# A recurrent mixer's decays from a second scan instead of reciprocals, and its conditioning vectors multiplied on VectorE

## The chip, the cores and the metric

The kernel runs on one core of one Trainium2 chip and computes a whole two-layer block in one launch. The metric is the device time of one execution in microseconds (us). Engines are named as in the profile: PE is TensorE's matmuls, PEld its weight loads, DVE is VectorE, ACT is ScalarE, POOL is GpSimd, SP is SyncE, which here only issues DMAs.

## What is computed

512 tokens of width 1024 pass through two layers, each with a mixer and a feed-forward part. The mixer of layer 0 is recurrent, that of layer 1 is dilated attention. Each layer has six conditioning vectors of 1024 numbers, `cond @ ada_w[layer] + ada_b[layer]`, which shift, scale and gate the norms. The parts that matter here:

```python
cond = jax.nn.silu(c)                                  # one row of 1024
mod = (cond @ ada_w[layer] + ada_b[layer])             # six vectors of 1024
sh1, sc1, g1, sh2, sc2, g2 = jnp.split(mod, 6, axis=-1)
u = rms_norm(h, norm_g[layer, 0]) * (1.0 + sc1) + sh1
# recurrent mixer, 8 heads of 128, chunks of C = 32 tokens
log_f = jnp.log(lb + (1.0 - lb) * jax.nn.sigmoid(f_raw))
k = (1.0 - lb) * jax.nn.sigmoid(-f_raw)
q = jax.nn.silu(q_raw)
b = jnp.cumsum(log_f, axis=2)                          # within a chunk
q_dec = q * jnp.exp(b)
k_inv = k * jnp.exp(-b)
a = jnp.where(causal, q_dec @ k_inv.T, 0.0)            # within a chunk
k_end = k * jnp.exp(b_last - b)                        # b_last: end of the chunk
o = a @ v + q_dec @ state
state = jnp.exp(b_last) * state + k_end.T @ v
o = rms_norm(o) * norm_g * silu(g)                     # per head
return o @ w_out
```

## The kernel before, in words

Matmuls with weights are done in fp32 precision from three products of rounded halves: each weight tile is split into `hi` (a cast on ACT, L113) and `lo` (raw minus hi on DVE, L114), and each tile of activations into `uh` and `ul`; the products uh·hi, ul·hi and uh·lo are L599, L600 and L601. One such matmul covers 128x512.

The weights come as one stream of 1 MB tiles called `raw` (class `Stream`), in an order fixed in the program. SP issues the loads in that order (L85). There are **two raw buffers**: the load of a tile waits until every reader of the tile two places ahead of it has finished. For a weight tile the readers are the hi cast and the lo subtraction; for a chunk of `ada_w` (512 of its rows by 512 columns, "conditioning chunk" below) they are whatever multiplies it with `cond`. The parts hi and lo have three buffers.

During the mixer of layer 0 the stream holds 12 weight tiles of the mixer (per pair of heads one of f, one of q, one of g) and, woven between them, 12 conditioning chunks of layer 0 (vectors 2, 3 and 4; each vector has two halves of 512 columns, each half two chunks: `ada_chunk(l, v, hf, kq)`), then the first chunks of layer 1. In the names of the trace and of the order below, raw0, 1, 3, 5, 9, 13, 15, 19, 23, 26, 30, 34 are the weight tiles f0, q0, f1, q1, g0, f2, q2, g1, f3, q3, g2, g3; raw2, 4 and 6, 8 are the two halves of vector 2, raw10, 12 and 14, 17 those of vector 4, raw18, 21 and 22, 25 those of vector 3; raw27 is the first chunk of layer 1.

`ada_groups` (L383 to L401) multiplies a chunk of layer 0 on PE: per chunk two records of four matmuls, each with a column tile of 32 (L395), 8 matmuls in all; after the second chunk ACT copies the sum from PSUM to `shared` (L399). Layer 1's chunks go the other way, `ada_chunk`'s own code: four DVE instructions per chunk (L415 for the first, L417 for the rest), each `shared += raw[:, k] * cond[k]`, 128x512. The sum over partitions is later made on PE with a column of ones (L444) and finished on DVE (L433, L435).

The mixer's loop goes over four pairs of heads. Per pair, `block` makes f and q (L599 to L601), ACT applies the sigmoids, then per head `head_prep` (L1503 to L1546) computes on DVE the decays inside chunks: a scan over 512 columns (L1510), the reciprocal of its 512 columns (L1516), products with K and Q (L1517 to L1519), 12 small steps of 4 or 16 elements (L1525 to L1536) and two products of 256 columns (L1542, L1543); two more products per head are on POOL (L1541, L1544). `core_a` to `core_d` (L1548 to L1603) are the head's matmuls; the output `on` of a head is written by DVE (L1595, tile aT) and transposed by PE in core_d (L1602). `gate_pair` makes g and multiplies the output (L1611, L1613). `fl` (Fillers) hands out these steps between blocks of the next weights, core_a to core_d two to five ticks behind `head_prep`.

The order on each engine is then set by a list scheduler with its own estimates of durations, not by hand; each engine runs its instructions in the order so fixed.

Of the kernel before, what the change touches and what calls it, by code (L numbers as in the profile page):

```python
# [37 lines left out]
SEEN = lambda t: t.rearrange("p (x n a) -> p x a n", a=2, n=P)  # L38
PLACED = lambda t: t.rearrange("p (x a n) -> p x a n", a=2, n=P)
# [276 lines left out]
def block_kernel(tc, x, c, positions, ada_w, ada_b, norm_g, hgrn_w_in, lower, hgrn_norm_g, hgrn_w_out,  # L316
                 attn_w_in, attn_w_out, ffn_w_in, ffn_w_out, inv_freq, out):
    nc = tc.nc
    act, dve, pool, pe = nc.scalar, nc.vector, nc.gpsimd, nc.tensor
    x2, out2 = x[0], out[0]  # L320
    V4 = lambda t: t.rearrange("p (a b) -> p a b", a=4)
# [3 lines left out]
    with ExitStack() as ctx:  # L325
# [48 lines left out]
        accs = {}  # L374
# [11 lines left out]
        def ada_groups(l, v, hf, kq):  # L386


            def run(raw):
                if kq == 0:  # L390
                    accs[l, v, hf] = bank("mm")
                ps, r = accs[l, v, hf], V4(raw)
                for k in range(4):
                    j = slice(32 * k, 32 * k + 32)
                    pe.matmul(ps[j], cond_tiles[:, kq * 4 + k], r[:, k], start=kq == 0, stop=kq == 1,  # L395
                              tile_position=(0, 32 * k))
                if kq == 1:
                    accs[l, v, hf] = acc_place()
                    act.copy(accs[l, v, hf], ps)  # L399
            return run  # L400
# [130 lines left out]
        one, two, own = ada_seq((1, 1)), ada_seq((1, 0)), ada_seq((0, 2), (0, 4), (0, 3), (1, 4))  # L531
# [54 lines left out]
        fl = Fillers()  # L586
# [774 lines left out]
        with tc.manual_schedule(engines=ORDERED):  # L1361
# [57 lines left out]
            tiles = list(vbanks)  # L1419
# [77 lines left out]
        head = sc.tile([P, S], F32, name="head")  # L1497
        pool.memset(head, 0.0)

        C16 = lambda a: a.rearrange("p (c t) -> p c t", t=32)  # L1500
        B44 = lambda a: a.rearrange("p (b c t) -> p b c t", b=4, c=4)

        def head_prep(hd, T, K, Q):  # L1503
            g = {}
            act.activation(T, T, AF.Identity, scale=omlb[:, hd:hd + 1], bias=lb[:, hd:hd + 1])
            act.activation(K, K, AF.Copy, scale=omlb[:, hd:hd + 1])
            dve.tensor_copy(C16(head)[:, :, 0:1], C16(T)[:, :, 0:1])
            dve.tensor_scalar(C16(T)[:, :, 0:1], C16(T)[:, :, 0:1], 0.0, None, op0=OP.mult)
            bb = fresh(sc, [P, S], "bb", 1)
            dve.tensor_tensor_scan(bb, T, head, 0.0, op0=OP.mult, op1=OP.add)  # L1510
# [4 lines left out]
            ke = T
            dve.reciprocal(ki, bb)  # L1516
            dve.tensor_mul(ki, ki, K)  # L1517
            dve.tensor_mul(qd, bb, Q)
            dve.tensor_tensor(C16(ke), C16(ki), dec.unsqueeze(2).broadcast_to((P, 16, 32)), op=OP.mult)  # L1519
            d4 = dec.rearrange("p (b c) -> p b c", c=4)  # L1520
            f = fresh(cp, [P, 4, 4], "fpre", 2)
            s = fresh(cp, [P, 4, 4], "fsuf", 2)
            tot = fresh(cp, [P, 4, 1], "ftot", 2)
            f64 = fresh(cp, [P, 4, 4], "f64", 2)
            dve.tensor_copy(f[:, :, 0:1], ones[:, 0:4].unsqueeze(2))  # L1525
            dve.tensor_copy(f[:, :, 1:2], d4[:, :, 0:1])
            dve.tensor_mul(f[:, :, 2:3], d4[:, :, 0:1], d4[:, :, 1:2])
            dve.tensor_mul(f[:, :, 3:4], f[:, :, 2:3], d4[:, :, 2:3])
            dve.tensor_copy(s[:, :, 3:4], ones[:, 0:4].unsqueeze(2))
            dve.tensor_copy(s[:, :, 2:3], d4[:, :, 3:4])  # L1530
            dve.tensor_mul(s[:, :, 1:2], d4[:, :, 2:3], d4[:, :, 3:4])
            dve.tensor_mul(s[:, :, 0:1], s[:, :, 1:2], d4[:, :, 1:2])
            dve.tensor_mul(tot, s[:, :, 0:1], d4[:, :, 0:1])
            dve.tensor_copy(f64, ones[:, 0:16].rearrange("p (b c) -> p b c", c=4))
            dve.tensor_copy(f64[:, :, 0:1], d4[:, :, 1:2])
            dve.tensor_copy(f64[:, :, 3:4], d4[:, :, 2:3])  # L1536
            bc = lambda a: a.unsqueeze(3).broadcast_to((P, 4, a.shape[2], 32))
# [3 lines left out]
            pool.tensor_tensor(B44(k128), B44(ke), bc(s), op=OP.mult)  # L1541
            dve.tensor_tensor(B44(m64)[:, :, 0:2], B44(ke)[:, :, 0:2], bc(f64[:, :, 0:2]), op=OP.mult)  # L1542
            dve.tensor_tensor(B44(m64)[:, :, 2:4], B44(qd)[:, :, 2:4], bc(f64[:, :, 2:4]), op=OP.mult)  # L1543
            pool.tensor_tensor(B44(q128), B44(qd), bc(f), op=OP.mult)  # L1544
            g.update(qd=qd, ki=ki, ke=ke, q128=q128, k128=k128, m64=m64, tot=tot, hd=hd)
            return g  # L1546
# [73 lines left out]
        for p in range(4):  # L1620
            tiles = []
            whi, wlo = st.take()
            for k in range(2):
                ps = block(whi, wlo, k * P, 256)
                T = fresh(sb, [P, S], "T", 3)
                K = fresh(sc, [P, S], "K", 2)
                act.activation(PLACED(T), SEEN(ps), AF.Sigmoid)
                act.activation(PLACED(K), SEEN(ps), AF.Sigmoid, scale=-1.0)
                tiles.append([T, K])
                fl.tick()  # L1630
            whi, wlo = st.take()
# [752 lines left out]
```

## Time and profile before

| | us |
|---|---|
| median of 3 runs | 1459.75 |
| fastest, slowest | 1458.21, 1462.43 |
| profiled execution, device time | 1458.26 |
| profiled execution, span of the trace | 1456.5 |

| engine | busy us | share of the span |
|---|---|---|
| PE | 1423.5 | 98% |
| PEld | 1309.1 | 90% |
| DVE | 1118.5 | 77% |
| ACT | 821.6 | 56% |
| POOL | 196.9 | 14% |

The table is an average over stages that differ: the mixer of layer 0 that the change touches lies between 74 and 260 us of the span. In a timeline a row is start, duration, engine, line, operation, `out<-in`, and in brackets the idle time of the engine just before it with what ended it. PE's matmuls overlap, so the distance between two starts, not the duration, is what one costs.

### The profile page before, as it was taken

The numbers are of one execution on the slowest core, as the hardware profiler recorded it, in microseconds if no ns is written. First come the engines' busy times: TensorE is split into PE (matmuls) and PEld (weight loads), VectorE is DVE, ScalarE is ACT, GpSimd is POOL, SyncE is SP. The second block draws the span as 40 slices with busy tenths as digits, with TensorE's granted clock in tenths as the row PEclk, the third lists the DMA queues.
The fourth block names the chain that finished last, engine by engine and source line by source line (L and its number), as shares of the span: only waits on it lengthen the run. The fifth ranks groups of instructions, "written<-read, shape, count | busy, mean of one in ns | idle before, by whom it ended". The sixth has DMA issues, their size and how long they took to land. (4 is left out here: it accounts for less than half of the span.)

```text
span 1456.5 us, 25346 instructions
## 1 busy us (share of the span) xinstructions
PE 1423.5 (98%) x9903; PEld 1309.1 (90%) x9903; DVE 1118.5 (77%) x1802; ACT 821.6 (56%) x1486; POOL 196.9 (14%) x173
## 2 busy tenths in 40 slices
PE   8999999999999999999999999999999999999998
PEld 6778888889999998888989999998998999999887
DVE  4588589478888889778797977888776978887644
ACT  4434433374555553366748878567895655555332
POOL 1012002040111103240000110001012211110100
PEclk9999999999999999999999999999999999999999
DMA  9656554213444358515244453254353334434541
GB/s 308 184 192 207 170 185 145 88 59 87 117 116 117 117 198 300 173 59 174 91 134 132 115 129 89 84 168 123 95 183 108 93 111 117 116 109 153 174 145 58
DMA packets 212873, 201.11 MB, mean 138 GB/s; under 512 B 8920, under 2 KB 170640, under 8 KB 212496
## 3 DMA queue, kind: packets, MB, share of 16 engines
q1 hardware_dynamic: 209776, 192.71, 42.6%
q10 hardware_dynamic: 1952, 6.65, 1.2%
q8 instruction: 78, 1.28, 0.4%
q0 software_dynamic: 1024, 0.12, 0.2%
q14 instruction: 43, 0.35, 0.1%
HBM read 192.30 MB, written 5.30 MB: 136 GB/s over the span
## 5 line engine op out<-in xcount | busy, mean ns | idle before, releaser
L1847 PE MATMUL ps_mm<-apart,hiq 128*128 128x256 f32 (+1 forms) x608 | 137.5, 320 | 3.4 <-ACT xs L1961 2.7
L599 PE MATMUL ps_mm<-uh,hi 128*128 128x512 f32 (+1 forms) x368 | 130.5, 355 | 0.0
L113 ACT CAST hi<-raw 128x2048 fp32r<-128x2048 f32 x39 | 74.3, 1906 | 98.5 <-DMA raw<-in_hgrn_w_in_dram 42.5
L600 PE MATMUL ps_mm<-ul,hi 128*128 128x512 f32 (+1 forms) x368 | 128.1, 348 | 1.6 <-DVE ul L699 1.6
L114 DVE TENSOR_TENSOR lo<-raw,hi 128x2048 fp32r<-128x2048 f32 x39 | 95.3, 2443 | 44.2 <-ACT hi L113 44.0
L601 PE MATMUL ps_mm<-uh,lo 128*128 128x512 f32 (+1 forms) x368 | 128.1, 348 | 0.0
L1847 PEld LDWEIGHTS ps_mm<-apart,hiq 128*128 128x128 f32 x608 | 99.9, 191 | 9.7 <-ACT xs L1961 3.3
L971 DVE TENSOR_TENSOR loq<-raw,hiq 128x1024 fp32r<-128x1024 f32 x72 | 84.9, 1221 | 20.1 <-ACT hiq L967 20.1
L980 PE MATMUL ps_mm<-th,hiq 128*128 128x256 f32 x360 | 99.1, 275 | 0.0
L980 PE MATMUL ps_mm<-th,loq 128*128 128x256 f32 x360 | 99.0, 275 | 0.0
L980 PE MATMUL ps_mm<-tl,hiq 128*128 128x256 f32 x360 | 99.0, 275 | 0.0
L1847 PE MATMUL ps_mm<-apart,loq 128*128 128x256 f32 (+1 forms) x304 | 95.4, 314 | 0.6 <-DVE loq L1983 0.6
L951 POOL TENSOR_TENSOR raw<-raw 128x512 f32<-128x512 f32 x36 | 47.8, 1329 | 320.1 <-DVE spare L947 165.0
L967 ACT CAST hiq<-raw 128x1024 fp32r<-128x1024 f32 x72 | 72.1, 1047 | 21.4 <-DVE raw L955 16.8
L599 PEld LDWEIGHTS ps_mm<-uh,hi 128*128 128x128 f32 x368 | 70.0, 190 | 12.4 <-issue 5.3
L600 PE MATMUL ps_mm<-lo,oh 128*128 128x512 f32 x208 | 78.9, 380 | 0.2 <-DVE lo L114 0.2
L599 PE MATMUL ps_mm<-hi,oh 128*128 128x512 f32 x208 | 79.0, 381 | 0.0
L600 PEld LDWEIGHTS ps_mm<-ul,hi 128*128 128x128 f32 x368 | 69.9, 190 | 9.3 <-DVE ul L699 2.0
L1083 ACT CAST oh<-mid 128x512 fp32r<-128x512 f32 x44 | 37.4, 872 | 69.4 <-PE ps_b L600 60.8
L601 PEld LDWEIGHTS ps_mm<-uh,lo 128*128 128x128 f32 x368 | 69.9, 190 | 6.8
L1847 PE MATMUL ps_mm<-uh,hiq 128*128 128x256 f32 x256 | 71.2, 278 | 0.2 <-ACT ps_mm L1936 0.2
L1847 PE MATMUL ps_mm<-uh,loq 128*128 128x256 f32 x256 | 70.4, 275 | 0.0
(477 smaller groups left out, 4783.4 us busy)
## 6 DMA issues: line engine op xcount, KB each, us to landing
raw<-in_ada_w_dram SPq DMA_DIRECT2D x40, 1024.0 KB, 5.9
raw<-in_ffn_w_in_dram SPq DMA_DIRECT2D x144, 256.0 KB, 4.1
raw<-in_ffn_w_out_dram SPq DMA_DIRECT2D x22, 1024.0 KB, 4.9
raw<-in_attn_w_in_dram SPq DMA_DIRECT2D x64, 256.0 KB, 4.3
raw<-in_hgrn_w_in_dram SPq DMA_DIRECT2D x12, 1024.0 KB, 5.4
raw<-in_attn_w_in_dram SPq DMA_DIRECT2D x12, 1024.0 KB, 5.2
raw<-in_ffn_w_in_dram SPq DMA_DIRECT2D x8, 1024.0 KB, 5.2
raw<-in_attn_w_in_dram SPq DMA_DIRECT2D x16, 512.0 KB, 5.0
```

Source lines behind the costliest of these rows:

```text
L113: self.nc.scalar.copy(hi, t)
L114: self.nc.vector.tensor_sub(lo, t, hi.bitcast(F32))
L599: pe.matmul(ps, ah, bh, start=start, stop=False, skip_group_check=part)
L600: pe.matmul(ps, ah, bl, start=False, stop=False, skip_group_check=part)
L601: pe.matmul(ps, al, bh, start=False, stop=stop, skip_group_check=part)
L951: pool.tensor_add(r[:, 2], r[:, 2], r[:, 0])
L967: act.copy(hi, src)
L971: dve.tensor_sub(lo, src, hi.bitcast(F32))
L980: pe.matmul(LAID(ps), w[x][:, a], TAKE(us[kt][y]), start=begin and kt + m == 0, stop=kt == 3 and m == 2, skip_group_check=True)
L1083: act.copy(PLACED(oh), SEEN(mid(f)))
L1847: pe.matmul(LAID(dst()), x, TAKE(y), start=begin and i == 0, stop=i == len(todo) - 1, skip_group_check=True)
```

## The change

Two parts. First, the 12 conditioning chunks of vectors 2, 3 and 4 of layer 0 are no longer multiplied on PE but on DVE, by the same code as layer 1's: 4 instructions per chunk, no ACT copy.

Second, `head_prep` becomes three functions. `decays` makes two scans of 528 columns per head in a layout of 33 columns a chunk, one forward (`bb`) and one from the back (`suf`, the decay from a position to the end of its chunk), so that `k_end` is `suf*K` and no 512-column reciprocal is needed. `between` does the small steps of both heads of a pair in one set, with a reciprocal of 2x16 columns. `widened` makes `ki` from `ke` and those reciprocals, and the four wide products as before (two on POOL). The sigmoid of f is written by ACT in two halves into the new layout. K has three buffers instead of two; the tile T with its three is replaced by two fixed tiles `factors`; POOL sets seven tiles at the mixer's start instead of one.

```diff
-        by_pe = lambda l, v, hf: l == 0 and v in (2, 3, 4)
-        sum_by_pe = lambda l, v, hf: by_pe(l, v, hf) or (l, v) == (1, 4) or (l, v, hf) == (1, 1, 0)
+        sum_by_pe = lambda l, v, hf: (l, v) in ((0, 2), (0, 3), (0, 4), (1, 4)) or (l, v, hf) == (1, 1, 0)
...
         def ada_chunk(l, v, hf, kq):
-            if by_pe(l, v, hf):
-                return ada_groups(l, v, hf, kq)
-
...
-        def head_prep(hd, T, K, Q):
...
+        def decays(hd, k, K, Q, dec):
+            T = factors[k]
+            act.activation(C33(T)[:, :, 1:33], C33(T)[:, :, 1:33], AF.Identity, scale=omlb[:, hd:hd + 1], bias=lb[:, hd:hd + 1])
             act.activation(K, K, AF.Copy, scale=omlb[:, hd:hd + 1])
+            bb, suf = fresh(sc, [P, 528], "bb", 1), fresh(sc, [P, 528], "suf", 1)
+            dve.tensor_tensor_scan(bb, T[:, 0:528], starts[:, 0:528], 0.0, op0=OP.mult, op1=OP.add)
+            dve.tensor_tensor_scan(suf[:, ::-1], T[:, 1:529][:, ::-1], starts[:, 1:529][:, ::-1], 0.0, op0=OP.mult, op1=OP.add)
+            dve.tensor_copy(dec[:, k], C33(bb)[:, :, 32])
             qd = fresh(sb, [P, S], "qd", 2)
+            dve.tensor_mul(C16(qd), C33(bb)[:, :, 1:33], C16(Q))
+            dve.tensor_mul(C16(K), C33(suf)[:, :, 1:33], C16(K))
+            return qd, K
+        def between(dec):
+            d = dec.rearrange("p k (b c) -> p (k b) c", c=4)
+            rdec = fresh(cp, [P, 2, 16], "rdec", 2)
+            dve.reciprocal(rdec, dec)
+            dve.tensor_copy(reach[:, :, 1:7:5], d[:, :, 0:4:3])
+            dve.tensor_mul(reach[:, :, 2:6:3], d[:, :, 0:3:2], d[:, :, 1:4:2])
+            dve.tensor_mul(reach[:, :, 3:5], reach[:, :, 2:6:3], d[:, :, 2:0:-1])
+            tot = fresh(cp, [P, 8, 1], "ftot", 2)
+            dve.tensor_mul(tot, reach[:, :, 4:5], d[:, :, 0:1])
+            dve.tensor_copy(f64[:, :, 0:4:3], d[:, :, 1:3])
+            return rdec, tot
+        def widened(hd, k, qd, ke, rdec, tot):
...
+            dve.tensor_tensor(C16(ki), C16(ke), rdec[:, k].unsqueeze(2).broadcast_to((P, 16, 32)), op=OP.mult)
...
-                act.activation(PLACED(T), SEEN(ps), AF.Sigmoid)
                 act.activation(PLACED(K), SEEN(ps), AF.Sigmoid, scale=-1.0)
+                for x in range(2):
+                    act.activation(C33(factors[k])[:, 8 * x:8 * x + 8, 1:33].rearrange("p (a c) t -> p a c t", a=2),
+                                   SEEN(ps)[:, x].rearrange("p a (c t) -> p a c t", t=32), AF.Sigmoid)
```

The order of SP's loads is the same before and after, and so is every engine's order behind the mixer. On DVE the scheduler places the new instructions between the mixer's. In the changed kernel's order L395 is the first and L397 the later multiplication of a chunk, L114 is lo as before, L1580 the output `on` of a head (L1595 before) and L1499, L1500 are the two scans.

DVE, between the outputs of head 0 (aT139) and head 1 (aT161), before:

```order
L1595 TENSOR_TENSOR aT139_1159<-ps_b138_1151,orr141_1165 128x512 [waits Pool_49]
L1529 COPY fsuf234_1735<-ones_74 128x4 [waits DVE_49]
L114 TENSOR_TENSOR lo15_1223<-raw15_1061,hi15_1222 128x2048 [waits DMAHW5_49,Activation_49]
L1611 TENSOR_TENSOR Q158_1253<-Q158_1253,ps_mm157_1228 128x512 [waits Activation_49]
L1613 TENSOR_TENSOR oT74_688<-oT74_688,Q158_1253 128x512 [waits DVE_49,Activation_49]
L613 TENSOR_SCALAR rv164_1277<-oss162_1271 128x4 [waits Activation_49]
L1525 COPY fpre233_1734<-ones_74 128x4 [waits Pool_49]
L1595 TENSOR_TENSOR aT161_1270<-ps_b160_1262,orr163_1276 128x512 [waits PE_49,Pool_49]
```

And the same stretch of DVE now (aT127, the output of head 0, is the row just ahead of it; aT150 is that of head 1):

```order
L395 TENSOR_SCALAR shared_97<-raw14_1032,cond_96 128x512 [waits DMAHW4_49]
L397 SCALAR_TENSOR_TENSOR shared_97<-raw14_1032,cond_96,shared_97 128x512 [waits DVE_49]
L1596 TENSOR_TENSOR Q147_1230<-Q147_1230,ps_mm146_1205 128x512 [waits Activation_49]
L397 SCALAR_TENSOR_TENSOR shared_97<-raw14_1032,cond_96,shared_97 128x512 [waits DVE_49] x2
L114 TENSOR_TENSOR lo15_1200<-raw15_1038,hi15_1199 128x2048 [waits DMAHW5_49,Activation_49]
L1598 TENSOR_TENSOR oT74_688<-oT74_688,Q147_1230 128x512 [waits Activation_49]
L593 TENSOR_SCALAR rv153_1254<-oss151_1248 128x4 [waits Activation_49]
L397 SCALAR_TENSOR_TENSOR shared_97<-raw17_1197,cond_96,shared_97 128x512 [waits DMAHW6_49,DVE_49]
L1596 TENSOR_TENSOR Q159_1292<-Q159_1292,ps_mm158_1267 128x512 [waits Activation_49]
L413 TENSOR_TENSOR cols_98<-ps_b164_1325,adab_95 128x4 [waits PE_49]
L397 SCALAR_TENSOR_TENSOR shared_97<-raw17_1197,cond_96,shared_97 128x512 [waits DVE_49]
L1580 TENSOR_TENSOR aT150_1247<-ps_b149_1239,orr152_1253 128x512 [waits Pool_49]
```

Raw14's four multiplications and two of raw17's now stand between the two outputs; raw17 is loaded into the buffer that raw14 leaves, and its first reader stands three rows behind lo15.

DVE, around the output of head 3, now (aT186; raw25 goes into the buffer that raw22 leaves):

```order
L395 TENSOR_SCALAR shared_97<-raw22_1348,cond_96 128x512 [waits DMAHW2_49]
L1529 TENSOR_TENSOR m64212_1669<-qd199_1599,f64_720 128x4x64 [waits DVE_49]
L415 SCALAR_TENSOR_TENSOR cols_98<-cols_98,smallB_94 128x4 [waits DVE_49]
L397 SCALAR_TENSOR_TENSOR shared_97<-raw22_1348,cond_96,shared_97 128x512 [waits DVE_49] x2
L593 TENSOR_SCALAR rv189_1543<-oss187_1537 128x4 [waits Activation_49]
L397 SCALAR_TENSOR_TENSOR shared_97<-raw22_1348,cond_96,shared_97 128x512 [waits DVE_49]
L397 SCALAR_TENSOR_TENSOR shared_97<-raw25_1486,cond_96,shared_97 128x512 [waits DMAHW4_49,DVE_49]
L1580 TENSOR_TENSOR aT186_1536<-ps_b185_1528,orr188_1542 128x512 [waits PE_49,Pool_49]
```

Before, no conditioning chunk of layer 0 was read by DVE, so none stood ahead of the output of head 3.

PE, around the transposes of head 0's output, now (the three-product matmuls continue on both sides):

```order
L1571 MATMUL ps_b149_1239<-v_tok_104,aT122_1093 128x128 [waits DVE_49,Activation_49]
L1571 MATMUL ps_b149_1239<-v_tok_104,aT122_1093 128x128
L1587 MATMUL ps_a148_1233<-ident_86,aT127_1136 128x128 [waits DVE_49,PE_49]
L1587 MATMUL ps_a148_1233<-ident_86,aT127_1136 128x128 x3
L1573 MATMUL ps_b149_1239<-state132_1151,q128108_956 128x128 [waits Pool_49]
```

The transposes of aT127 stand, as L1602 did before, at a fixed place in PE's order and wait for DVE's write of it; the L395 rows of before, which stood between such places, are gone from PE.

## Rows read from the trace of the kernel before

**Rows 1.** Page, its head and its line of busy times
```profile
span 1456.5 us, 25346 instructions
PE 1423.5 (98%) x9903; PEld 1309.1 (90%) x9903; DVE 1118.5 (77%) x1802; ACT 821.6 (56%) x1486; POOL 196.9 (14%) x173
```

**Rows 2.** Windows of the mixer: stretch, length, busy time and instructions by engine
```profile
74.00:140.00 66.00, 65.61 (x384) 51.35 (x377) 56.06 (x115) 25.34 (x41) 12.23 (x10) 1.00 0.61 202
140.00:199.00 59.00, 59.00 (x406) 48.91 (x404) 42.38 (x80) 22.14 (x52) 8.97 (x8) 1.00 0.51 163
199.00:247.00 48.00, 46.11 (x288) 40.88 (x287) 42.37 (x80) 16.05 (x36) 8.73 (x6) 0.96 0.47 152
```

**Rows 3.** Timeline of PE, one chunk's matmuls between weight matmuls
```profile
84.86 0.38 PE L600 MATMUL ps_mm<-ul,hi 128*128 128x512 f32 x1
85.07 0.38 PE L601 MATMUL ps_mm<-uh,lo 128*128 128x512 f32 x1
85.38 1.06 PE L395 MATMUL ps_mm<-raw,cond_tiles 128*32 128x512 f32 x8
86.38 0.48 PE L599 MATMUL ps_mm<-uh,hi 128*128 128x512 f32 x1
```

**Rows 4.** Lines of DVE from 74 to 262 us: busy us, mean ns, idle before
```profile
L114 DVE TENSOR_TENSOR lo<-raw,hi 128x2048 fp32r<-128x2048 f32 x12 | 27.5, 2290 | 21.4 <-ACT hi L113 21.4
L1516 DVE RECIPROCAL ki<-bb 128x512 f32<-128x512 f32 x8 | 26.8, 3344 | 0.0
L417 DVE SCALAR_TENSOR_TENSOR shared<-raw,cond,shared 128x512 f32<-128x512 f32 x21 | 15.5, 738 | 2.6 <-DMA raw<-in_ada_w_dram 2.4
L1510 DVE TENSOR_TENSOR_SCAN bb<-T,head 128x512 f32<-128x512 f32 x8 | 11.5, 1432 | 0.1
```

**Rows 5.** Timeline of DVE, single instructions
```profile
82.68 1.22 DVE L1510 TENSOR_TENSOR_SCAN bb<-T,head 128x512 f32<-128x512 f32 x1
...
87.31 0.16 DVE L1527 TENSOR_TENSOR fpre<-dec 128x4 f32<-128x4 f32 x1
87.38 0.17 DVE L1530 COPY fsuf<-dec 128x4 f32<-128x4 f32 x1
...
197.61 3.10 DVE L417 SCALAR_TENSOR_TENSOR shared<-raw,cond,shared 128x512 f32<-128x512 f32 x4
```

**Rows 6.** DMA issues from 74 to 262 us: KB each, median us to landing
```profile
raw<-in_ada_w_dram SPq DMA_DIRECT2D x17, 1024.0 KB, 5.1
raw<-in_hgrn_w_in_dram SPq DMA_DIRECT2D x9, 1024.0 KB, 5.4
```

**Rows 7.** Timeline of SP's queue, the load of raw15
```profile
132.21 0.37 SPq L85 DMA_DIRECT2D raw<-in_hgrn_w_in_dram  x1
```

**Rows 8.** Timeline of ACT, the hi cast of raw15 and a copy of a state
```profile
137.70 1.90 ACT L113 CAST hi<-raw 128x2048 fp32r<-128x2048 f32 x1 [5.05 <-DMA raw<-in_hgrn_w_in_dram]
...
206.31 0.27 ACT L1574 COPY state<-ps_b 128x128 f32<-128x128 f32 x1
```

**Rows 9.** Timeline of DVE, an output, two waits and the state step behind one
```profile
138.27 0.69 DVE L1595 TENSOR_TENSOR aT<-ps_b,orr 128x512 f32<-128x512 f32 x1
...
176.30 2.29 DVE L114 TENSOR_TENSOR lo<-raw,hi 128x2048 fp32r<-128x2048 f32 x1 [5.10 <-ACT hi L113]
...
211.90 0.75 DVE L417 SCALAR_TENSOR_TENSOR shared<-raw,cond,shared 128x512 f32<-128x512 f32 x1 [2.36 <-DMA raw<-in_ada_w_dram]
212.57 0.34 DVE L1576 SCALAR_TENSOR_TENSOR state<-state,ftot,ps_b 128x128 f32<-128x128 f32 x1
```

**Rows 10.** Timeline of PE: core_d of head 0, f3's first block, a wait, g3's first block
```profile
139.71 0.27 PE L1602 MATMUL ps_a<-ident,aT 128*128 128x128 f32 x1
...
198.98 0.46 PE L599 MATMUL ps_mm<-uh,hi 128*128 128x512 f32 x1
...
226.29 0.91 PE L444 MATMUL ps_b<-ones,shared 128*128 128x1 f32 x7 [1.50 <-DVE T L1508]
...
247.04 0.46 PE L599 MATMUL ps_mm<-uh,hi 128*128 128x512 f32 x1
```

**Rows 11.** Window of 3 us behind that wait; column after the counts: granted clock
```profile
228.00:231.00 3.00, 3.00 (x17) 3.00 (x16) 2.93 (x5) 0.69 (x1) 1.90 (x1) 0.52 0.02 8
```

More of the change, by code (lines that the diff above doesn't have):

```diff
@@ L381, in acc_place @@
             return shared[:, 2 + turns_of_acc[0] % 2]
-        by_pe = lambda l, v, hf: l == 0 and v in (2, 3, 4)
-        sum_by_pe = lambda l, v, hf: by_pe(l, v, hf) or (l, v) == (1, 4) or (l, v, hf) == (1, 1, 0)
[L386 to L400, printed above, removed]
+        sum_by_pe = lambda l, v, hf: (l, v) in ((0, 2), (0, 3), (0, 4), (1, 4)) or (l, v, hf) == (1, 1, 0)
         def ada_chunk(l, v, hf, kq):
-            if by_pe(l, v, hf):
-                return ada_groups(l, v, hf, kq)
             def run(raw):
@@ L1496, in block_kernel @@
         pool.affine_select(causal, ones, [[1, P]], OP.is_ge, 0.0, base=0, channel_multiplier=-1)
-        head = sc.tile([P, S], F32, name="head")
-        pool.memset(head, 0.0)
+        C33 = lambda a: a[:, 0:528].rearrange("p (c t) -> p c t", t=33)
+        starts = sc.tile([P, 529], F32, name="starts")
+        factors = [sc.tile([P, 529], F32, name=f"factors{k}") for k in range(2)]
+        for t in (starts, *factors):
+            pool.memset(t, 0.0)
+        pool.memset(C33(starts)[:, :, 0:1], 1.0)
@@ L1500, in block_kernel @@
+        pool.memset(starts[:, 528:529], 1.0)
+        reach = sc.tile([P, 8, 8], F32, name="reach")
+        pool.memset(reach, 1.0)
+        f64 = sc.tile([P, 8, 4], F32, name="f64")
+        pool.memset(f64, 1.0)
         C16 = lambda a: a.rearrange("p (c t) -> p c t", t=32)
         B44 = lambda a: a.rearrange("p (b c t) -> p b c t", b=4, c=4)
-        def head_prep(hd, T, K, Q):
-            g = {}
-            act.activation(T, T, AF.Identity, scale=omlb[:, hd:hd + 1], bias=lb[:, hd:hd + 1])
+        bc = lambda a: a.unsqueeze(3).broadcast_to((P, 4, a.shape[2], 32))
@@ L1506, in head_prep @@
+        def decays(hd, k, K, Q, dec):
+            T = factors[k]
+            act.activation(C33(T)[:, :, 1:33], C33(T)[:, :, 1:33], AF.Identity, scale=omlb[:, hd:hd + 1], bias=lb[:, hd:hd + 1])
             act.activation(K, K, AF.Copy, scale=omlb[:, hd:hd + 1])
[L1507 to L1510, printed above, removed]
@@ L1511, in head_prep @@
-            dec = fresh(cp, [P, 16], "dec", 2)
-            dve.tensor_copy(dec, C16(bb)[:, :, 31])
-            qd = fresh(sb, [P, S], "qd", 2)
-            ki = fresh(sc, [P, S], "ki", 2)
[L1515 to L1537, printed above, removed]
+            bb, suf = fresh(sc, [P, 528], "bb", 1), fresh(sc, [P, 528], "suf", 1)
@@ L1538, in head_prep @@
+        def widened(hd, k, qd, ke, rdec, tot):
+            own = slice(4 * k, 4 * k + 4)
+            ki = fresh(sc, [P, S], "ki", 2)
+            dve.tensor_tensor(C16(ki), C16(ke), rdec[:, k].unsqueeze(2).broadcast_to((P, 16, 32)), op=OP.mult)
             q128 = fresh(cp, [P, S], "q128", 2)
@@ L1540, in head_prep @@
             m64 = fresh(sc, [P, S], "m64", 2)
[L1541 to L1546, printed above, removed]
+            pool.tensor_tensor(B44(k128), B44(ke), bc(reach[:, own, 4:8]), op=OP.mult)
+            dve.tensor_tensor(B44(m64)[:, :, 0:2], B44(ke)[:, :, 0:2], bc(f64[:, own, 0:2]), op=OP.mult)
+            dve.tensor_tensor(B44(m64)[:, :, 2:4], B44(qd)[:, :, 2:4], bc(f64[:, own, 2:4]), op=OP.mult)
+            pool.tensor_tensor(B44(q128), B44(qd), bc(reach[:, own, 0:4]), op=OP.mult)
+            return dict(qd=qd, ki=ki, ke=ke, q128=q128, k128=k128, m64=m64, tot=tot[:, own], hd=hd)
         def core_a(g):
@@ L1624, in block_kernel @@
                 ps = block(whi, wlo, k * P, 256)
-                T = fresh(sb, [P, S], "T", 3)
-                K = fresh(sc, [P, S], "K", 2)
-                act.activation(PLACED(T), SEEN(ps), AF.Sigmoid)
+                K = fresh(sb, [P, S], "K", 3)
                 act.activation(PLACED(K), SEEN(ps), AF.Sigmoid, scale=-1.0)
-                tiles.append([T, K])
+                for x in range(2):
+                    act.activation(C33(factors[k])[:, 8 * x:8 * x + 8, 1:33].rearrange("p (a c) t -> p a c t", a=2),
+                                   SEEN(ps)[:, x].rearrange("p a (c t) -> p a c t", t=32), AF.Sigmoid)
+                tiles.append([K])
                 fl.tick()
@@ L1638, in block_kernel, with first_steps @@
                 if k == 1:
+                    pair = {}
+                    def first_steps(tiles=tiles, p=p, pair=pair):
+                        dec = fresh(cp, [P, 2, 16], "dec", 2)
+                        pair["of"] = [decays(2 * p + i, i, *tiles[i], dec) for i in range(2)]
+                        pair["by"] = between(dec)
+                    fl.add(fl.n, first_steps)
                     for i in range(2):
@@ L1641, in block_kernel @@
                         g = {}
-                        fl.add(n, lambda g=g, a=(2 * p + i, *tiles[i]): g.update(head_prep(*a)))
+                        fl.add(n, lambda g=g, i=i, p=p, pair=pair: g.update(widened(2 * p + i, i, *pair["of"][i], *pair["by"])))
                         fl.add(n + LAG, lambda g=g: core_a(g))
```

## Prediction

> **What bounds the kernel now.** I read the busy line first [rows 1]: PE is busy 98% of the span, DVE 77%. That is an average, so next come the windows of the mixer, the only stage that the change touches [rows 2]. There PE is full (65.6 of 66 us, 59.0 of 59, 46.1 of 48) and its weight loads are not far behind (51.4, 48.9, 40.9), while DVE is busy 56.1, 42.4 and 42.4. So PE bounds the mixer today and DVE has about 10, 17 and 6 us to spare. The reader should note how small the first and third figure are. The other views tell how tightly DVE and PE already mesh: the output of head 0 is written by DVE at 138.27 for 0.69 us and its transposes start on PE at 139.71 [rows 9, 10], a slack of 0.75 us; and DVE already waits for loads, 5.10 us for a hi cast at 176.30 and 2.36 us for a conditioning chunk at 211.90 [rows 9]. In that second wait the state step behind it had been ready since ACT's copy at 206.31 to 206.58 [rows 8], and it still ran only at 212.57 [rows 9]: **DVE does not pass over a row that waits**.
>
> **PE loses the 12 chunks.** The eight matmuls of a chunk put the next weight matmul at 86.38 where, at the pitch of 84.86 to 85.07, it would have come at 85.28 [rows 3]: 1.1 us a chunk, 12 x 1.1 = 13 us in all. All 12 lie before 199 us. That is the whole possible gain on the bounding engine, and it is the upper end of it.
>
> **DVE, what it loses.** Per head the 512-column reciprocal of 3.34 us goes [rows 4], and the second scan comes at about 1.22 us [rows 5]: 8 x 2.1 = 17 us less. The three wide products stay three (suf·K, bb·Q, K·rdec), as do the two of 256 columns and POOL's two. Small steps: 15 per head become 8 per pair; 88 fewer, at the pitch of 0.07 us of a run of them [rows 5] 6 us. Together 23 us less, 2.85 per head.
>
> **DVE, what it gains.** 48 multiplications of 128x512 at 0.74 [rows 4], 0.78 in a dependent run of four [rows 5]: 35 us, 2.95 a chunk. Net DVE is 12 us busier; by its total that would vanish in the slack. By window it does not. Chunks raw2 to raw12 fall in the first one, with three to four heads: 56.1 + 6 x 2.95 - 3.5 x 2.85 = 64 of 66 us, where PE needs 65.6 - 6 x 1.1 = 59. In the second, 42.4 + 17.7 - 9 = 51 against PE's 52. So **DVE, not PE, is the longer engine of the first window, and level in the second**, before any wait.
>
> **The waits that the change adds.** DVE runs its instructions in the order fixed. A chunk used to leave its raw buffer when PE had read it; now when its fourth multiplication has come up in DVE's row. Only then does SP issue the load two places on, 5.1 us to landing for a chunk, 5.4 for a weight tile [rows 6] (raw15: issued 132.21, its cast starts 137.70 [rows 7, 8]), and a weight's lo also waits for the 1.90 us cast [rows 8]. Where DVE has less than that between the last reader and the first user, it must idle, whatever else is going on. From the rows of the changed order, with 0.69 for a 512-column product, 0.74 for a multiplication and 2.29 for a lo:
> - raw14 to raw17: three rows between, 2.29 + 0.69 + small = 3, so about 2.5 us idle, and the output of head 1 (aT150) stands behind it.
> - raw21 to lo23: 5.4 + 1.9 = 7.3 less two products and two steps of 128 columns, 2: about 5.5 us, and head 2's output (aT175) stands behind it.
> - raw22 to raw25: nothing between: 5.4 us, and head 3's output (aT186) is the very next row.
> - raw7 to lo9 1.5, raw10 to raw12 about 1, raw12 to raw14 2.7, raw25 to raw27 2.
>
> Walking DVE's and PE's new rows with these durations, side by side: PE would reach the transposes of head 0 at about 134.5 instead of 139.7, but aT127 is written only by 140.0, so PE waits 5.3 us and the 5 us gained so far are gone. Further waits: head 1 2.2; a state 1.2; aT175 0.7 (most of DVE's 5.5 lies beside PE's weight matmuls); a column sum that DVE must read out 2.2; aT186 5.7. Sum up to the first block of f3 (198.98 before [rows 10]): 17.3 against 13, with PE's work before that place otherwise equal: 4.3 later. From there to g3's first block (247.04) another 2.1 + 0.9 + 2.8 = 5.8, while the wait of 1.50 at 226.29 goes [rows 10]: 4.3 more. After that wait the granted clock stood at 0.52 for the 3 us from 228 [rows 11], 1.4 us lost. That loss goes with its wait, and the larger new waits may bring others, of which the next wait for DVE swallows a part: together nothing here, up to 7 in the last rival. 4.3 + 4.3 = 8.6; I walked each row as strictly late, so I round down to **+8 us**. 1458.26 + 8 = 1466, after the profiled execution, whose own time is 1.5 under the median; I name 1466 for the median too.
>
> **Costed at nothing.** The six ACT copies that go and the eight extra sigmoid starts: ACT is busy 16 to 25 us of each window [rows 2], that idle time is the cover; without it, eight starts of a few tenths. POOL's six more memsets: POOL is busy 12.2 of 66 us over 10 instructions [rows 2], so by that mean 1.2 each, 7 us, in idle time; uncovered, they would come once, in front of the first sigmoid. The weights: their loads now come later, but f3's lo was done at 178.6 and its first block came at 198.98 [rows 9, 10], 20 us early; 8 us of it can go before a block waits.
>
> **Bounds of the unknown.** No row shows a scan that runs backwards. Lower bound the cost of a plain 512-column product, 0.69 [rows 9], upper the reciprocal's 3.34; I take the forward scan's 1.22, the nearest in kind. Eight of them: from -4 to +17 us of DVE, of which about half would reach PE (the rest fills waits for loads): -2 to +8. The 32-column reciprocal: between 0.16 of a small step [rows 5] and 3.34 of the wide one; I take the wide one's share, 3.34/16, four times: nothing. The scans of before took 1.43 on the mean against 1.22 at 82.68 [rows 4, 5]; what lengthens some may fall on other instructions now, 16 scans by 0.2 either way, ±3.
>
> **The rivals.**
> *PE stays the bound (faster).* The new DVE waits fall beside PE work that can go on, because several weight blocks lie between any two places where PE needs a head. For it: PE has 98% and DVE had 23% free [rows 1]; DVE's 5.1 us wait at 176.30 held PE up nowhere. Against: the 0.75 us of slack at head 0, and that each output stands behind the chunk's loads. It gives 1458.3 - 13 = 1445 in full, 1452 if half is eaten. The Trainium skill ("Perfetto Trace Analysis", Identifying the Most-Contended Engine) says to optimize the engine with the highest occupancy first; by that rule relieving PE pays, here by those 13 us. The row agrees that PE is that engine; only the windows speak against it. Chance 0.25.
> *It cancels.* The waits eat just what PE saves: within 4 us of 1460. For: most single waits of my walk are 2 to 3 us, and half of any of them could be mistaken. Chance 0.19.
> *DVE paces the mixer (the forecast).* Decided where the sum of DVE's added waits before its outputs exceeds 13 us; my sum is 17 by 199 us and about 22 by 247. 1464 to 1475. Chance 0.48.
> *Worse.* The reversed scan is dear, or the clock stays at half behind each of five waits over 2 us: 5 x 1.4 = 7 on top, 1473 to 1485. Chance 0.08.
>
> The Trainium skill ("TensorE: Matmul & The Clock Gate", on the engines' queues) calls VectorE's queue strictly first in, first out, where TensorE may pull weight loads ahead. The trace agrees. With a DVE that could step over such a row, the time would be the first rival's 1445.
>
> **How the numbers follow.** Likeliest is the forecast, 1466. A measurement of this kernel tells about 0.3% from no change, 4.4 us, so faster means under 1455.4 and slower over 1464.1. Faster: the first rival, 0.25. Same: cancelling, 0.19. Slower: 0.48 + 0.08 = 0.56. Range: down to 1450, which takes in the half-eaten gain and leaves out the full one (about 0.1); up to 1477, which takes in the unknown scan's likelier half and leaves out 0.07. The forecast's own range is 1464 to 1475.
>
> **What would show it.** Right: in the first two windows DVE is busier than before by some 8 us each and PE below 95%; PE's idle time is named for DVE's aT (the outputs) and states; DVE's idle time for chunk and hi releases, 5 us before aT186 among them; f3's first block comes near 203, g3's near 255; behind the mixer both traces run in parallel. Wrong: f3's first block before 195 with PE full, then the first rival holds; reversed scans over 2 us, then the price of them is wrong, not the waits; a weight's cast that holds PE, then the margin of the loads was misread.

## The result and the profile after

| | before, us | after, us | ratio (95% interval) |
|---|---|---|---|
| median of 20 runs each | 1459.67 | 1465.32 | 1.0034 (1.0027 to 1.0042) |
| span of the profiled execution | 1456.5 | 1462.1 | |
| mean granted clock of the execution | 0.997 | 0.993 | |

The change made the kernel slower by 5.6 us; that is small, but the interval of the ratio lies wholly above 1. (Ratios, here and below, are of all the runs and not of the two medians, which would give 1.0039.) The forecast was +6 on the median (1466) and +8 on the profiled execution. The first lines of the page answer to [rows 1]:

```profile
span 1462.1 us, 25107 instructions
PE 1416.2 (97%) x9807; PEld 1310.4 (90%) x9807; DVE 1128.2 (77%) x1762; ACT 817.3 (56%) x1488; POOL 198.9 (14%) x179
```

DVE's share is 77% as before and PE's is one point lower; from this page alone nobody would see a reason for the loss. The windows that answer to [rows 2] (stretch, length, then PE, PEld, DVE, ACT and POOL busy, clock, DMA share, GB/s) show where to look:

```profile
74.00:140.00 66.00, 59.12 (x329) 50.79 (x327) 58.93 (x89) 21.99 (x41) 14.02 (x15) 0.99 0.51 167
140.00:199.00 59.00, 54.33 (x317) 47.13 (x316) 47.19 (x74) 18.77 (x48) 9.73 (x8) 0.92 0.49 162
199.00:247.00 48.00, 47.19 (x325) 41.91 (x323) 41.93 (x68) 20.18 (x42) 8.22 (x6) 1.00 0.60 198
```

PE was full in the first two windows and now idles 6.9 and 4.7 us in them, and in the second the clock fell from 1.00 to 0.92. The waits of PE between 74 and 255 us, by what ended them (us in total, times, longest):

```profile
PE ps_b L1571 <- DVE state L1561: 4.7, 1, 4.7
PE ps_b L424 <- DVE shared L397: 3.3, 1, 3.3
PE ps_b L424 <- DVE cols L413: 2.6, 1, 2.6
PE ps_b L1557 <- ACT k L1551: 2.0, 2, 1.3
PE ps_b L442 <- DVE shared L397: 1.5, 1, 1.5
```

With the five small ones not shown they make 15.2 us, against 2.3 us before (1.50, 0.39 and 0.39). Three places of PE, which answer to [rows 10] (core_d of head 0, f3's first block, g3's first block):

```profile
140.08 1.06 PE L1587 MATMUL ps_a<-ident,aT 128*128 128x128 f32 x4
...
202.96 0.46 PE L579 MATMUL ps_mm<-uh,hi 128*128 128x512 f32 x1
...
251.07 0.46 PE L579 MATMUL ps_mm<-uh,hi 128*128 128x512 f32 x1
```

So PE is 4.0 us late at f3 and 4.0 at g3, and 5.7 at the first transposes of the next norm (304.17 before, 309.89 after). From there the two traces run in parallel. What was lost besides waits stands in the clock column of four stretches behind three long waits of PE (which ended at 139.10, 190.02 and 250.16; the second and the third stretch belong to one wait):

```profile
140.00:144.00 4.00, 4.00 (x22) 3.84 (x21) 2.79 (x5) 0.00 (x0) 1.00 (x1) 0.71 0.83 281
190.00:195.00 5.00, 4.98 (x16) 4.35 (x17) 4.82 (x9) 0.00 (x0) 2.69 (x2) 0.51 0.00 1
195.00:200.00 5.00, 5.00 (x25) 4.26 (x24) 3.69 (x7) 0.83 (x1) 0.00 (x0) 0.81 0.72 217
250.00:255.00 5.00, 4.84 (x18) 4.08 (x19) 2.83 (x7) 0.95 (x1) 0.00 (x0) 0.66 0.96 335
```

PE is busy in all four and does less: 4 x 0.29 + 5 x 0.49 + 5 x 0.19 + 5 x 0.34 = 6.3 us of matmul time lost, against 1.4 before [rows 11]. The account then closes to within a microsecond: -13.0 for the chunks, +12.9 of waits, +4.9 of clock is +4.8, measured 5.7 at the end of the mixer.

### The profile page after: what moved, and what is told of

Read it like the earlier page. It is cut to its first block, busy times and chain, and to the rows that moved or that the text cites. A ratio compares the mean times of both kernels' runs of the same rounds, so it can differ in the third digit from the quotient of the medians.

```text
span 1462.1 us, 25107 instructions
## 1 busy us (share of the span) xinstructions
PE 1416.2 (97%) x9807; PEld 1310.4 (90%) x9807; DVE 1128.2 (77%) x1762; ACT 817.3 (56%) x1488; POOL 198.9 (14%) x179
## 3 DMA queue, kind: packets, MB, share of 16 engines
q8 instruction: 77, 1.26, 0.4%
## 5 line engine op out<-in xcount | busy, mean ns | idle before, releaser
L114 DVE TENSOR_TENSOR lo<-raw,hi 128x2048 fp32r<-128x2048 f32 x39 | 95.3, 2443 | 42.3 <-ACT hi L113 42.3
L397 DVE SCALAR_TENSOR_TENSOR shared<-raw,cond,shared 128x512 f32<-128x512 f32 x112 | 88.7, 794 | 12.8 <-DMA raw<-in_ada_w_dram 11.4
L947 ACT CAST hiq<-raw 128x1024 fp32r<-128x1024 f32 x72 | 72.1, 1046 | 20.8 <-DVE raw L935 16.2
```

What stands on the lines that cost most here:

```text
L114: self.nc.vector.tensor_sub(lo, t, hi.bitcast(F32))
L947: act.copy(hi, src)
```

## The experiments

The changed kernel differs from the one before in two parts, so the first four runs take them apart. Two things hold for all runs. The list scheduler sets the order anew for each kernel, so a run shows its edit together with the order that the edit led to. And the kernel before ran again beside each group of runs, with medians from 1458.07 to 1459.67; differences to the changed kernel are therefore taken from the ratios to the kernel before.

**scans_only: the new decays, all chunks on PE.**

```diff
+        by_pe = lambda l, v, hf: l == 0 and v in (2, 3, 4)
...
         def ada_chunk(l, v, hf, kq):
+            if by_pe(l, v, hf):
+                return ada_groups(l, v, hf, kq)
```

> The changed kernel with the 12 conditioning chunks back on PE (8 matmuls a chunk, ACT copies), the new decays kept. Theory (the chunks on DVE make its row late, the new decays do not): PE has its 13 us of chunk matmuls back, DVE loses the 35 us of multiplications, so DVE is busy about 45 us of the first mixer window and PE waits for it nowhere for more than 1.5 us; time 1456 to 1460, ratio to before 0.997 to 1.000, granted clock near 0.997. Rival A (the new decays are late, because both heads' steps are done in one set before either head can go on): the waits of 3 to 5 us for states, column sums and chunks stay, time 1462 or more.

Measured: 1454.63 us, ratio to before 0.9974 (0.9963 to 0.9986). PE's waits are 1.9 us in all, the longest 1.1, and the clock is 1.00 in all three windows:

```profile
74.00:140.00 66.00, 65.64 (x379) 51.69 (x376) 45.04 (x62) 25.70 (x45) 10.21 (x15) 1.00 0.61 199
140.00:199.00 59.00, 58.63 (x411) 49.28 (x410) 39.63 (x65) 22.28 (x54) 8.75 (x8) 1.00 0.55 179
199.00:247.00 48.00, 46.89 (x301) 41.99 (x300) 40.54 (x64) 19.69 (x41) 8.11 (x6) 1.00 0.50 175
```

Rival A falls: the decays by themselves are a gain of 4 us, a little more than the theory said. The same places of PE show where: f3's first block 1.0 us earlier than before, g3's 4.0 (243.08), the next norm 4.0 (300.21). Three of the four come where the kernel before had its wait of 1.50 us and the 1.4 us of half clock behind it [rows 10, 11].

**ada_only: the old decays, all chunks on DVE.**

```diff
-            if by_pe(l, v, hf):
-                return ada_groups(l, v, hf, kq)
```

> The kernel before with the 12 chunks on DVE and the old head_prep with its 512-column reciprocals. Theory: DVE would be busy 56 + 18 = 74 us in the first window of 66 and 60 of 59 in the second, so the heads' outputs come 8 to 10 us later than in the changed kernel and the time is 1474 to 1490. Rival A (the new decays make the waits): without them the time is that of PE without its 13 us, 1445 to 1455.

Measured: 1466.98 us, ratio 1.0044 (1.0029 to 1.0060). Both expectations missed. The direction is the theory's, so the chunks alone make the kernel slower; but 12 chunks with 23 us more of DVE work cost hardly more than with less. DVE is at 62.8 of 66 and 53.1 of 59 us there, and only 43.3 of 48 in the third window. Summing DVE's work by window was too strict: the wait of PE ahead of head 0's transposes is no longer than in the changed kernel (4.37 us instead of 4.69), it only ends later (at 142.75 instead of 139.10).

| | chunks on PE | chunks on DVE |
|---|---|---|
| reciprocals (before) | 1 | 1.0044 |
| two scans | 0.9974 | 1.0034 (the change) |

The chunks cost 0.4 to 0.6% in either row although they take 13 us from PE; the scans give 0.3% in the first column and 0.1% in the second, where the two intervals overlap.

**v3_on_dve and v2_on_dve: four chunks on DVE.** From scans_only, with

```diff
-        by_pe = lambda l, v, hf: l == 0 and v in (2, 3, 4)
+        by_pe = lambda l, v, hf: l == 0 and v in (2, 4)
```

and `(3, 4)` for the second.

> The changed kernel with vectors 2 and 4 back on PE and only vector 3 (four chunks, raw18 to raw25) on DVE. Theory: PE loses 4 x 1.1 = 4.4 us; DVE in the first window carries no chunk (45 of 66 us), in the second 42 + 12 - 9 = 45 of 59, so PE waits for DVE less than 2 us in all; time 1454 to 1458, ratio 0.996 to 0.999. Rival B (what costs is a few places where a product of POOL beside DVE's steps makes a column sum late, whatever the load): the wait of 2.6 us at the first column sum of the third pair and the half clock behind it stay, time 1459 to 1463.

> The changed kernel with vectors 3 and 4 back on PE and only vector 2 (four chunks at the mixer's start, raw2 to raw8) on DVE. Theory: PE loses 4.4 us; DVE in the first window 56 + 12 - 10 = 58 of 62 us, nearly as long as PE, so a part is waited for: 1455 to 1460, ratio 0.997 to 1.000. Rival A: as in the changed kernel, 1462 or more.

Measured: 1456.23 (0.9984, 0.9975 to 0.9994) and 1457.12 (0.9986, 0.9977 to 0.9995). Both times fall in the theory's range, its reason did not hold: with 4.4 us less on PE neither is faster than scans_only (the medians are higher, the intervals overlap). With vector 3 on DVE, PE waits 7.6 us, 5.4 of them in the third window; with vector 2 there is a wait that I had not thought of, PE itself standing 4.5 us for a chunk whose load had to wait for vector 2's multiplications, and a clock of 0.55 in the 6 us from it on:

```profile
116.07 1.93 PE L395 MATMUL ps_mm<-raw,cond_tiles 128*32 128x512 f32 x8 [4.52 <-DMA raw<-in_ada_w_dram]
```

**half_v3: two chunks on DVE.** From scans_only:

```diff
-        by_pe = lambda l, v, hf: l == 0 and v in (2, 3, 4)
+        by_pe = lambda l, v, hf: l == 0 and (v in (2, 4) or (v, hf) == (3, 0))
```

> The kernel with the new decays and only the second half of vector 3 (two chunks, raw22 and raw25) on DVE, ten chunks on PE. Theory: PE loses 2.2 us and DVE has room there (40 of 59 us), waits as in the kernel with no chunk on DVE: 1452 to 1454.5, ratio 0.995 to 0.997. Rival: any chunk on DVE costs what it saves, 1454 to 1457.

Measured: 1464.22 us (1.0032, 1.0019 to 1.0045), far outside. The trace read here is of the slowest of its 12 runs (1466.71). Until the column sum ahead of f3 it is 0.7 us behind scans_only (197.84 against 197.13). Then PE waits 2.75 us at 239.64 and again here:

```profile
250.48 0.59 PE L444 MATMUL ps_b<-ones,shared 128*128 128x1 f32 x2 [3.33 <-DVE shared L417]
```

This is the changed kernel's wait of 3.3 us at 250.16 again. What PE waits for is the last chunk of layer 1 that the mixer multiplies, which no edit here touches. SP's queue shows why it is late. The loads of raw23, raw25, raw26 and the next two chunks, in scans_only and then in half_v3:

```profile
167.92 0.37 SPq L85 DMA_DIRECT2D raw<-in_hgrn_w_in_dram  x1
168.78 0.37 SPq L85 DMA_DIRECT2D raw<-in_ada_w_dram  x1
177.44 0.37 SPq L85 DMA_DIRECT2D raw<-in_hgrn_w_in_dram  x1
184.01 4.47 SPq L85 DMA_DIRECT2D raw<-in_ada_w_dram  x2
```

```profile
169.94 0.37 SPq L85 DMA_DIRECT2D raw<-in_hgrn_w_in_dram  x1
179.40 0.37 SPq L85 DMA_DIRECT2D raw<-in_ada_w_dram  x1
185.22 0.37 SPq L85 DMA_DIRECT2D raw<-in_hgrn_w_in_dram  x1
197.15 1.03 SPq L85 DMA_DIRECT2D raw<-in_ada_w_dram  x2
```

With PE reading raw22, its buffer is free at 168.78 for raw25; with DVE reading it, raw25 waits for lo23, until 179.40. Everything behind in the stream is late with it: layer 1's first chunk is loaded 13 us later (184.01 and 197.15; 198.72 in the changed kernel), and the last multiplication of its last chunk here comes at 249.69 instead of 236.38 (249.36 in the changed kernel). So **two chunks on DVE delay every later load of the stream**, and a price falls 50 us behind them, on a column sum that had no wait before. The late loads are not all of it: four of DVE's steps between 241.09 and 245.96, ahead of that last multiplication, are 2.6 us longer than the same steps in no_pool (next run), and there the column sum does not wait, though these loads come at 193.19, 9 us behind scans_only. With all four chunks of vector 3 on DVE (v3_on_dve) these loads come at 191.23 and that last multiplication at 239.47, and the column sum does not wait, so the number of chunks alone does not decide it.

**no_pool: POOL's wide products left out.**

```diff
-            q128 = fresh(cp, [P, S], "q128", 2)
-            k128 = fresh(sb, [P, S], "k128", 2)
+            q128, k128 = still[k], still[2 + k]
...
-            pool.tensor_tensor(B44(k128), B44(ke), bc(reach[:, own, 4:8]), op=OP.mult)
...
-            pool.tensor_tensor(B44(q128), B44(qd), bc(reach[:, own, 0:4]), op=OP.mult)
```

> The changed kernel without POOL's 16 wide products: k128 and q128 are two constant tiles each instead of products, so the states and the outputs hold other numbers; everything else is computed as before. Theory C (POOL's products beside DVE's steps stretch those: between 185.9 and 191.5 us four steps of DVE took 1.2 to 1.5 us instead of 0.4 to 0.7, about 3.4 us more, just ahead of the column sum for which PE waits 2.6 us and behind which the clock is at half): DVE's m and qd steps take 0.42 and 0.69 everywhere, that wait and the half clock behind it go, time 1456 to 1461. Rival D (the load of the chunks alone makes DVE late): less than 2 us gained, 1463 to 1466.

Measured: 1453.59 us (0.9959, 0.9945 to 0.9974), 0.75% or 10.9 us under the changed kernel and more than expected. The same stretch of DVE's order, after and then in no_pool (start, duration):

```profile
185.56 0.41 DVE L1528 TENSOR_TENSOR m<-K,f 128x256 f32<-128x256 f32 x1
185.89 1.28 DVE L1529 TENSOR_TENSOR m<-qd,f 128x256 f32<-128x256 f32 x1
187.09 1.26 DVE L1528 TENSOR_TENSOR m<-K,f 128x256 f32<-128x256 f32 x1
188.28 1.53 DVE L1503 TENSOR_TENSOR qd<-bb,Q 128x512 f32<-128x512 f32 x1
```

```profile
183.44 0.41 DVE L1529 TENSOR_TENSOR m<-K,f 128x256 f32<-128x256 f32 x1
183.77 0.42 DVE L1530 TENSOR_TENSOR m<-qd,f 128x256 f32<-128x256 f32 x1
184.11 0.42 DVE L1529 TENSOR_TENSOR m<-K,f 128x256 f32<-128x256 f32 x1
184.44 0.69 DVE L1506 TENSOR_TENSOR qd<-bb,Q 128x512 f32<-128x512 f32 x1
```

And POOL beside the first of the two:

```profile
185.84 1.05 POOL L1527 TENSOR_TENSOR k<-K,reach 128x512 f32<-128x512 f32 x1 [5.18 <-DVE reach L1514]
186.84 1.23 POOL L1530 TENSOR_TENSOR q<-qd,reach 128x512 f32<-128x512 f32 x1
188.04 1.22 POOL L1527 TENSOR_TENSOR k<-K,reach 128x512 f32<-128x512 f32 x1
```

The three DVE steps that meet a POOL product are 0.84 to 0.86 us longer, the short ones as much as the long one. It is not always DVE that gives way: the lo that starts at 133.43 together with a POOL product keeps its 2.28 us, and there the product takes 3.18. The three longer steps, 2.5 us in all, made the step at 189.81 late, for which PE waited 2.63 us at a column sum, and behind that wait lies the largest loss of clock. In no_pool that wait is gone and the one of 4.69 us has become 2.44; another of 2.65 us, for ACT, stands at 196.22. So the 10.9 us are the lengthening and POOL's place in the heads' chain together; this run does not part them.

**side1: one raw buffer more, for the chunks.**

```diff
         LAG = 2
         fl.n = 0
+        st.aside, st.asides = cx.enter_context(tc.tile_pool(name="m_more", bufs=1)), 1
```

(with `self.asides` in place of the number 2 in `Stream`, and `st.aside = None` ahead of the fourth pair)

> The changed kernel with one more raw buffer during the first three pairs of the mixer, kept for chunks and bias rows, so that a weight's load no longer waits for a chunk's multiplications. Theory E (raw buffers held by chunks pace DVE: 15.6 us idle before lo for hi casts): DVE's idle time before lo falls below 8 us, PE's waits halve, time 1456 to 1461. Rival D (DVE's row is full and in the wrong order whatever the loads do): 1463 to 1467.

Measured: 1456.74 us (0.9987, 0.9976 to 0.9998), 6.9 us under the changed kernel. Between 74 and 255 us DVE's idle time before lo falls from 15.6 to 4.9 us, its idle time for chunks rises from 8.9 to 14.6, as they now share one buffer; PE's waits fall from 15.2 to 11.5 only. Theory E holds in its time, not in its halving.

**lag3: the heads' matmuls one tick later.**

```diff
-        LAG = 2
+        LAG = 3
```

> The changed kernel with the heads' matmuls one tick later (LAG 3 instead of 2), about 5 us of weight matmuls more between a head's steps on DVE and their use on PE. Theory (PE waits because DVE's steps are late by 2 to 5 us): the waits for states and outputs go, those for column sums stay; time 1457 to 1462. Rival F (the heads' tiles have two buffers, so what PE uses later DVE may write later): no gain or a loss, 1464 to 1470.

Measured: 1459.34 us (1.0010, 0.9995 to 1.0024), 3.5 us under the changed kernel. The waits for states and outputs did not go: they are more in number and shorter, the longest 1.64 us instead of 4.69.

**pool384, side1_pool384 and scans_pool384: POOL's products only where they are read.** Block 0 of q128 and block 3 of k128 are read by nothing.

```diff
-            pool.tensor_tensor(B44(k128), B44(ke), bc(reach[:, own, 4:8]), op=OP.mult)
+            pool.tensor_tensor(B44(k128)[:, 0:3], B44(ke)[:, 0:3], bc3(reach[:, own, 4:8][:, 0:3]), op=OP.mult)
```

(q128 with `1:4` likewise; once on the changed kernel, once on side1, once on scans_only)

> The changed kernel with POOL's 16 wide products over the three blocks of 128 columns that are read, not four (block 3 of k128 and block 0 of q128 are used by nothing). Theory C (POOL's products stretch DVE's steps): a quarter less of POOL, so about a quarter of the 12 us that leaving them out gave: 1461 to 1463.5. Rival D: 1464 to 1467.

> The changed kernel with both: the extra raw buffer for chunks and POOL's products over three blocks. If the two causes add (8.6 us for the buffer, 2 to 3 for POOL): 1452 to 1456. Rival (one hides the other): 1456 to 1459.

> All 12 chunks on PE, the new decays, POOL's products over three blocks. Theory: PE is full and waits for DVE less than 2 us already, so little is left: 1453 to 1455, as without the narrower products. Rival (POOL is worth something by itself): under 1452.5.

Measured: 1461.14 (1.0010, 0.9999 to 1.0021), 1453.88 (0.9963, 0.9951 to 0.9976) and 1454.28 (0.9969, 0.9957 to 0.9980), all three as the theory had them. The two causes, buffer and POOL, add: 6.9 and 3.5 us by themselves, 10.4 together.

**side1_mix: the extra buffer, POOL's narrower products, and of each vector one half on DVE.**

```diff
-        by_pe = lambda l, v, hf: l == 0 and v in (2, 3, 4)
+        by_pe = lambda l, v, hf: l == 0 and v in (2, 3, 4) and hf == 0
```

> The new decays, the extra raw buffer, POOL's products over three blocks, and of each vector the first half (two chunks) on PE, the second on DVE: six chunks on DVE. Theory (waits, not work, eat the gain): PE loses 6.6 us, DVE gains half as much as in the changed kernel, waits under 4 us with their half clock: 1449 to 1454. Rival (any chunk on DVE costs what it saves): 1454 to 1458.

Measured: 1468.34 us (1.0059, 1.0047 to 1.0071), the highest median of all (its interval overlaps that of ada_only). PE waits 14.0 us, the longest 3.89 at 115.80 for a masked product of DVE, and the first window has a clock of 0.92; DVE itself stands 9.3 us once for ACT's decay factors. Here DVE is not full (44.3 of 66 us). Why the order came out so badly was not followed further.

Of the versions that compute the whole block, six lie under both kernels with their whole interval. The lowest are side1_pool384, with all chunks on DVE, and scans_pool384 and scans_only, with none, some 4 to 5 us under the kernel before. Their intervals overlap, so none is shown to be the best: with the buffer and the narrower products the chunks on DVE cost nothing that can be measured, but no run shows a gain from the 13 us taken from PE.

## Why the prediction was right

**Direction and size.** +8 us on the profiled execution was forecast, +5.6 measured. The rival that PE stays the bound needed f3's first block before 195 with PE full; it came at 202.96.

**Head 0.** Held nearly to the number. PE ran out of work at 134.4 (134.5 in the prediction), DVE wrote the output from 139.21 to 139.89 (140.0), core_d started at 140.08, and the wait was 4.69 us (5.3). But the step that ended it is another one:

```profile
139.10 1.19 PE L1571 MATMUL ps_b<-v_tok,aT 128*128 128x128 f32 x4 [4.69 <-DVE state L1561]
```

PE waited at the matmuls just ahead of the transposes, for a state step of DVE (138.62 to 138.96) that stands two rows ahead of the output. The cause, DVE's row being late, is the prediction's; the place is not.

**The other waits of PE up to f3.** The walk had them wrong. Head 0 and the column sum took 4.69 and 2.63 us, together 7.3 (7.5 walked). At the other four places, head 1, a state, aT175 and aT186, 9.8 us were walked, and PE waited 0.2 us or less at each. Another 3.7 us stood where the walk had nothing: 1.51 at the column sum at 109.17, 0.67, 1.32 and 0.21 for ACT at 116.15, 163.91 and 201.80. Of the sign that PE's idle time would be named for DVE's outputs and states, the states came true (4.9 us); the outputs themselves (aT) account for 0.2 us.

**DVE's busy sums.** Too high by 5 us in the first window (64 predicted, 58.9 measured), and by 4 in the second. By work DVE was not the longer engine of the first window: PE has 59.1 us there and DVE 58.9. That DVE held PE up rests on the order of its row and on its own waits.

**The waits of DVE for loads.** raw21 to lo23 was walked as 5.5 us and stood at 5.56. Others came close or smaller (lo9 1.95 for 1.5; raw12 1.02 for 1; raw14 1.25 for 2.7; raw17 0.79 for 2.5, since lo15 ahead of it had already waited 1.53; raw27 did not wait, for 2). The prediction's 5.4 us for **raw22 to raw25 did not exist**, and the text ahead of it is wrong on the buffer. These rows of the changed kernel show the 5.56 us, the load of raw25, and the last multiplication of raw22 with the first of raw25:

```profile
177.13 2.29 DVE L114 TENSOR_TENSOR lo<-raw,hi 128x2048 fp32r<-128x2048 f32 x1 [5.56 <-ACT hi L113]
...
193.10 1.54 DVE L397 SCALAR_TENSOR_TENSOR shared<-raw,cond,shared 128x512 f32<-128x512 f32 x2
```

```profile
179.45 0.37 SPq L85 DMA_DIRECT2D raw<-in_ada_w_dram  x1
```

The load was issued at 179.45, the moment lo23 ended (177.13 + 2.29 = 179.42). So raw25 took the buffer of raw23, not of raw22, whose last multiplication ended at about 193.9, when the load of raw26 was issued (193.88): the two buffers do not strictly take turns. In DVE's row lo23 stands ahead of the multiplications of raw22, so raw23's buffer came free first; how the scheduler chooses is not shown. The step that failed is "nothing between: 5.4 us", and with it the 5.7 us of PE's wait for head 3's output.

**The clock.** Another failing term, of the other sign. It was set to nothing in the sum and up to 7 in the last rival; it was +4.9. Up to f3 the walk summed 17.3 us of waits; measured are 11.6 of waits and 4.6 of half clock, together 16.2. The total was right because errors of both signs nearly cancel, and that was luck.

**From f3 to g3.** Predicted 4.3 us later, measured 0: of 5.8 us of waits only 3.33 and 0.31 came, and the old wait and its half clock went. The 1.7 us that the half clock took behind g3's wait came on top.

**The unknown prices.** The reversed scan takes 1.24 us and the forward one 1.25, both over 528 columns, so the forward scan was the right row to take. The 32-column reciprocal takes 0.35, above the 0.21 by its share of the wide one. What lengthened some of the scans of before, priced at ±3 us without a cause, is POOL: two of the eight scans met a POOL product (this one started at 180.13) and took 2.07 and 2.08 us, the other six 1.21 to 1.22:

```profile
180.37 2.08 DVE L1510 TENSOR_TENSOR_SCAN bb<-T,head 128x512 f32<-128x512 f32 x1
```

In the changed kernel no scan is lengthened, other steps are. The ±3 us were too little as a weight for this: without POOL's products the changed kernel is 10.9 us faster, though the kernel before has the same 16 of them.

**The rule on the most contended engine.** The Trainium skill ("Perfetto Trace Analysis", Identifying the Most-Contended Engine) would have relieved PE. Here that cost 5.6 us, since the work went to an engine which PE waits for in order. The measurement decides against the rule taken by the kernel's average.

## What to carry to other kernels

When work moves from the engine that is full to one that is three quarters busy, read the second engine's order around what the first waits for, not its share: 13 us taken from PE came back as 13 us of waits and 5 us of half clock behind them. A wait of the matmul engine can have a second price in its clock, as the three longest had here. It need not: in v3_on_dve PE waited 2.69 and 2.38 us in the third window, and the granted clock stayed at 1.00. Nor are many short waits shown to be cheaper than a few long ones: lag3 has them shorter, and its three windows have clocks of 0.97, 0.98 and 0.96. And a buffer held longer by a slow reader delays the whole stream behind it: look for the price not only where the reader stands but at the last item of the stream (50 us later in half_v3, where POOL's products had a share in the price).

The wait of 2.69 us and the third window of v3_on_dve (granted clock: third column from the end):

```profile
213.00 0.49 PE L1593 MATMUL ps_b<-state,q 128*128 128x128 f32 x2 [2.69 <-DVE state L1581]
```

```profile
199.00:247.00 48.00, 42.48 (x278) 37.52 (x277) 41.71 (x67) 17.00 (x38) 8.57 (x6) 1.00 0.60 198
```

## What was not expected of the hardware

A POOL product over 128x512 (1.05 to 1.23 us) lengthened the DVE steps with two SBUF inputs that started beside it at 185.89, 187.09 and 188.28 by about 0.85 us each: a 128x256 product took 1.26 to 1.28 us beside it and 0.41 to 0.42 without, a 128x512 one 1.53 and 0.69. Over the mixer the multiplications of chunks averaged 798 ns with POOL's products and 746 without. The Trainium skill ("GPSIMD Engine Reference", Specifications) says that POOL shares its SBUF interfaces with VectorE and contends with instructions of two SBUF inputs; the trace agrees, with 0.85 us as the price in these rows. A step of one input was lengthened too: in the kernel before a copy of 128x4 took 1.02 us at 132.10, beside a POOL product that started at 131.46, and 0.16 in the median of its eight. And the granted clock fell behind single waits of 2.6 to 4.7 us: to 0.51 over 5 us behind the one of 2.63, and to 0.71 over 4 us behind the one of 4.69; behind the 2.69 us of v3_on_dve it did not fall.
